# Token halves in one 512-column pass, and two heads of an attention unit issued side by side

## The chip, the cores and the metric

The kernel runs as one launch on one core of a Trainium2 chip. The metric is the device time of that launch in microseconds (us): the median of several runs, lower is better. A difference of about 0.2% (4.6 us) is what a measurement of this kernel can tell from no change.

## The reference

The reference is a small network on 256 tokens of width 1024, all in float32: two layers of a first block, then one layer of a second block. What the change touches is shown; the second block's recurrent mixer is left out.

```python
def swiglu(x, w_gate, w_up, w_down):                       # D_FF = 2816
    return (jax.nn.silu(x @ w_gate) * (x @ w_up)) @ w_down

def first_block(x, ...):
    for layer in range(2):
        x = x + 0.5 * swiglu(rms_norm(x, norm_ffn1[layer]), ...)
        xn = rms_norm(x, norm_mix[layer])
        # 16 heads of 64; layer 0: 8 heads stick-breaking, 8 heads softmax with rotary q, k
        # layer 1: 8 heads softmax with a forgetting term, 8 heads dilated windows with rotary q, k
        mixed = mix(xn, ...)                                # q, k, v = split(xn @ w_in)
        x = x + mixed @ w_out[layer]
        x = x + 0.5 * swiglu(rms_norm(x, norm_ffn2[layer]), ...)
    return x

def peer_ffn(h, w_q, sub_keys, expert_u, expert_v):         # second block, 16384 experts
    ...                                                     # gate, eidx: 8 heads x top 16 of the experts
    act = gelu(einsum('nhed,nd->nhe', expert_u[eidx], hb))
    return einsum('nhe,nhed->nd', gate * act, expert_v[eidx])
```

## The kernel before

Activations lie transposed: a tile `x` of 128 partitions x 8 chunks x 256 tokens. Every large float32 product is made of three passes in the type fp32r: each operand is split into a high part and the remainder, and high x high, high x low and low x high are added up in PSUM. The normalised activations are two tiles, `xnh` and `xnl`; the weights are brought from memory in blocks of 128 x 512 (256 KB) by `wblk`, which loads `wr`, makes `wh` on ScalarE (L195) and `wl` on VectorE or GpSimd (L201). Four blocks rotate, in some stages five.

`ws` is the work horse: for each 128 x 128 weight tile it issues the three passes L224, L225, L226, each with 256 token columns. It serves

- `ffn`, four times: 22 steps of gate and up (both in one PSUM tile `mm`, a "pair" of 2 x 256 columns), evicted by one VectorE multiply with the norm's factor (L297), then SiLU, a multiply and a split into `hh`, `hl`; then 8 output chunks of 22 weight tiles each, evicted by one VectorE instruction (L304);
- `mix`, twice: eight "units" of two heads, in two groups of four. `project` makes q and k of a unit, `heads` normalises and rotates them, `weights` makes scores and softmax (or the stick-breaking weights), `collect` turns the weights round and multiplies by the values. The loop runs them with lags of 1, 2 and 3 units, so that a unit's stages lie beside the projection of later units; `values` makes v once for each group, in passes of 512 columns (L205 to L207);
- `to_x`, the output projection of `mix`, in two parts so that its first half lies beside the last units;
- the 128 steps of the expert stage's `u_phase` (PSUM tile `pu`), 64 of which lie beside the 24 passes of a `v_phase` (L1302 to L1304).

The code gives each engine's work, but a scheduler sets the order on each engine, by its own estimate of when each instruction can run; an instruction under `keep_in_program_order` stays behind the one written before it. Each engine then works its list in order and waits where an operand or a buffer isn't ready. In `mix`, PSUM is four `mm` buffers of one bank and four `w` buffers of one bank, which all attention tiles share in turn (scores, transposes, the two head helpers, the output `O`).

In the attention, head `e` of a unit sits on partitions 64e to 64e + 63 of q and k, so that a score matmul uses 64 of the array's 128 rows; in the product with the values, head `e` fills output partitions 64e to 64e + 63, which is 64 of its columns. These matmuls are plain float32; the profile records each as two.

## Time and profile before

| | |
|---|---|
| median of 3 runs | 2279.07 us (2274.92 to 2279.41) |
| the profiled execution | 2276.94 us, of which the span from first to last instruction 2275.2 us |
| TensorE matmul (PE) busy | 2196.3 us, 97% of the span, 18034 records |
| VectorE (DVE) busy | 1617.6 us, 71% |
| ScalarE (ACT) busy | 1346.1 us, 59% |
| GpSimd (POOL) busy | 283.0 us, 12% |
| mean granted TensorE clock | 0.99 of 2.4 GHz |
| moved by DMA | 365.30 MB, mean 161 GB/s |

Matmul records overlap: one of 256 columns is recorded with some 0.28 us, but the next starts 0.12 us later. So the price of a pass is read from the distance of starts, not from its record, and "busy" on PE also covers short waits.

By stages, in us from the start: first feed-forward 0 to 201, first mix 201 to 343, two feed-forwards 343 to 724, second mix 724 to 870, feed-forward 870 to 1065, the second block's mixer to 1350, its expert stage to 2230, the rest to 2275.

### The profile page before, as it was taken

Reading aid. Unit: us, or ns where it says so; the run is one execution under the profiler, and the core shown is the slowest. Engines: PE = TensorE matmul, PEld = TensorE weight load, DVE = VectorE, ACT = ScalarE, POOL = GpSimd, SP = SyncE. Lnnn points to the kernel's source line nnn. Section 1 sums busy time; section 2 is a strip of 40 time slices with the busy share of each in tenths; the row PEclk is TensorE's granted clock in tenths of the full one; section 3 lists DMA queues with packets and bytes.
Section 4 is the critical chain, followed back from the end, with each engine's and each line's share of the span. In section 5 each row is a group of like instructions: output and inputs, shape, how many; then the busy total and the mean of one; then the engine's idle time right before and its main releaser. Section 6 shows DMA issues by size and latency. Waiting matters only on the chain.

```text
span 2275.2 us, 48212 instructions
## 1 busy us (share of the span) xinstructions
PE 2196.3 (97%) x18034; PEld 2114.0 (93%) x18034; DVE 1617.6 (71%) x3293; ACT 1346.1 (59%) x2667; POOL 283.0 (12%) x272
## 2 busy tenths in 40 slices
PE   8999999999999999999888989889999999999997
PEld 8999889999999789999787889889999999999997
DVE  7766777666766757766886577999996666666666
ACT  6555576556555556556765656456665555555556
POOL 1001100000000101001233027960000000000001
PEclk9999999999999999999998999999999999999999
DMA  6566425565567325565243145443346555555553
GB/s 208 183 181 193 125 94 192 183 183 187 184 179 223 116 83 173 183 181 185 86 134 113 47 156 172 149 140 112 121 144 206 185 185 186 183 189 189 187 186 117
DMA packets 209659, 365.30 MB, mean 161 GB/s; under 512 B 31056, under 2 KB 39312, under 8 KB 208912
## 3 DMA queue, kind: packets, MB, share of 16 engines
q1 hardware_dynamic: 207312, 361.96, 50.4%
q8 instruction: 141, 2.31, 0.4%
q14 instruction: 94, 0.77, 0.1%
q10 hardware_dynamic: 2112, 0.26, 0.1%
HBM read 357.87 MB, written 4.26 MB: 159 GB/s over the span
## 4 chain that ended last, share of the span: by engine, by line
PE 82%; DVE 9%; ACT 3%; DMA 2%; POOL 2%; issue 2%; SPq 0%; DVEq 0%; POOLq 0%; ACTq 0%
PE mm L224 13%; PE mm L226 13%; PE mm L225 13%; PE acc L1302 5%; PE acc L1304 5%; PE acc L1303 5%; PE pu L225 5%; PE pu L224 5%; PE pu L226 5%; DVE wl L201 2%; PE pg L1282 2%; POOL wl L201 1%; DMA wr<-in_pu 1%; PE w L347 1%; PE mm L205 1%
## 5 line engine op out<-in xcount | busy, mean ns | idle before, releaser
L195 ACT ACTIVATE wh<-wr 128x512 fp32r<-128x512 f32 (+1 forms) x1348 | 836.4, 624 | 697.0 <-PE mm L225 240.5
L201 DVE TENSOR_TENSOR wl<-wr,wh 128x512 fp32r<-128x512 f32 (+1 forms) x1234 | 851.6, 696 | 485.5 <-ACT wh L195 455.7
L224 PE MATMUL mm<-xnh,wh 128*128 128x256 f32 x1840 | 529.2, 288 | 10.6 <-ACT wh L195 7.3
L226 PE MATMUL mm<-xnh,wl 128*128 128x256 f32 x1840 | 524.4, 285 | 1.6 <-POOL wl L201 0.9
L225 PE MATMUL mm<-xnl,wh 128*128 128x256 f32 x1808 | 514.7, 285 | 0.1
L224 PEld LDWEIGHTS mm<-xnh,wh 128*128 128x128 f32 x1840 | 355.0, 193 | 15.1 <-ACT wh L195 11.4
L226 PEld LDWEIGHTS mm<-xnh,wl 128*128 128x128 f32 x1840 | 355.0, 193 | 3.9 <-POOL wl L201 1.5
L225 PEld LDWEIGHTS mm<-xnl,wh 128*128 128x128 f32 x1808 | 349.1, 193 | 2.7 <-issue 1.9
L226 PE MATMUL pu<-xnh,wl 128*128 128x256 f32 x1024 | 291.2, 284 | 11.1 <-POOL wl L201 10.6
L224 PE MATMUL pu<-xnh,wh 128*128 128x256 f32 x1024 | 292.9, 286 | 0.0
L225 PE MATMUL pu<-xnl,wh 128*128 128x256 f32 x1024 | 289.6, 283 | 0.0
L1302 PE MATMUL acc<-o,wh 128*128 128x256 f32 x1024 | 286.9, 280 | 0.0
L1304 PE MATMUL acc<-o,wl 128*128 128x256 f32 x1024 | 285.8, 279 | 0.0
L1303 PE MATMUL acc<-o,wh 128*128 128x256 f32 x1024 | 285.7, 279 | 0.0
L226 PEld LDWEIGHTS pu<-xnh,wl 128*128 128x128 f32 x1024 | 195.6, 191 | 13.2 <-POOL wl L201 12.5
L226 PE MATMUL mm<-hh,wl 128*128 128x256 f32 x704 | 197.8, 281 | 0.0
L224 PE MATMUL mm<-hh,wh 128*128 128x256 f32 x704 | 197.1, 280 | 0.0
L224 PEld LDWEIGHTS pu<-xnh,wh 128*128 128x128 f32 x1024 | 196.0, 191 | 0.0
L225 PEld LDWEIGHTS pu<-xnl,wh 128*128 128x128 f32 x1024 | 195.8, 191 | 0.0
L225 PE MATMUL mm<-hl,wh 128*128 128x256 f32 x704 | 195.7, 278 | 0.0
L1304 PEld LDWEIGHTS acc<-o,wl 128*128 128x128 f32 x1024 | 192.4, 188 | 0.1
L1302 PEld LDWEIGHTS acc<-o,wh 128*128 128x128 f32 x1024 | 192.5, 188 | 0.0
(458 smaller groups left out, 3897.7 us busy)
## 6 DMA issues: line engine op xcount, KB each, us to landing
wr<-in_ffn_gu SPq DMA_DIRECT2D x352, 256.0 KB, 2.9
wr<-in_pu SPq DMA_DIRECT2D x256, 256.0 KB, 2.9
wr<-in_pv SPq DMA_DIRECT2D x256, 256.0 KB, 2.9
wr<-in_ffn_d SPq DMA_DIRECT2D x160, 256.0 KB, 2.8
wr<-in_qk SPq DMA_DIRECT2D x64, 256.0 KB, 3.0
wr<-in_wo SPq DMA_DIRECT2D x48, 256.0 KB, 2.9
wr<-in_v SPq DMA_DIRECT2D x32, 256.0 KB, 2.8
wr<-in_u_g SPq DMA_DIRECT2D x32, 256.0 KB, 2.7
```

The costliest lines, as they stand in the source:

```text
L195: nc.scalar.activation(wh[:, :n], wr[:, :n], AF.Copy)
L201: (self.nc.gpsimd if eng == "p" else self.nc.vector).tensor_sub(out, a, b)
L205: nc.tensor.matmul(out, lh, rh, start=start, stop=False)
L224: self.nc.tensor.matmul(out, wh[:, s], h, start=first, stop=False, **kw)
L225: self.nc.tensor.matmul(out, wh[:, s], l, start=False, stop=False, **kw)
L226: self.nc.tensor.matmul(out, wl[:, s], h, start=False, stop=last, **kw)
L347: nc.tensor.matmul(O[s, 0:T], vtok[:, 0, hv * 64:hv * 64 + 64], PT[:, 0:256], start=True, stop=False)
L1282: nc.tensor.matmul(pg[:, j], o[0][:, j], o[1][:, j], start=True, stop=True)
L1302: nc.tensor.matmul(o, vh[:, s], ph, start=first, stop=False, skip_group_check=True)
L1303: nc.tensor.matmul(o, vh[:, s], pl, start=False, stop=False, skip_group_check=True)
L1304: nc.tensor.matmul(o, vl[:, s], ph, start=False, stop=last, skip_group_check=True)
```

## The change

1. `xnh` and `xnl` become the two halves of one tile `xn2`, as `hh` and `hl` become `h2`: for each chunk the 256 high columns and the 256 low columns lie next to each other. A new `ws2` sends both through the array in one pass of 512 columns with the weight tile `wh`, and adds `wl` x high as a pass of 256 columns into the second half of the sum. Three passes become two.
2. The sum then stands in two halves of a PSUM bank; `merged` adds them at eviction: ScalarE copies the second half out, VectorE adds the first half to the copy. Gate/up tiles become `wide` ones of two banks, two in turn instead of four.
3. `ws2` serves gate/up, seven of eight output chunks of each feed-forward, the q and k projections, and 72 of the 128 `u_phase` steps. In the feed-forward the norm's factor goes onto the gate alone and, as `rsh`, onto the output.
4. In `mix`, the score matmuls of a unit's two heads are written in turn (`scores2`), the products with the values too (`pv2`), the transposes head after head (`turn`); all but the first of each series are pinned behind the one before. The transposes become a stage of their own, first in the loop.
5. `to_x` of the first block takes its accumulators from the two wide tiles, four chunks in each; the gates of the second layer and the feed-forward's output chunks use `w` tiles.

```diff
+    def ws2(self, out, src, x2, nk):
+        for b in range(0, nk, self.wk):
+            n = min(self.wk, nk - b)
+            wh, wl = self.wblk(src[:, b * 128:(b + n) * 128], n * 128)
+            for k in range(n):
+                s = slice(k * 128, k * 128 + 128)
+                both = x2[:, b + k].rearrange("p a t -> p (a t)")
+                last = b + k == nk - 1
+                if last:
+                    self.nc.tensor.matmul(out[:, T:], wl[:, s], x2[:, b + k, 0], start=False, stop=False)
+                self.nc.tensor.matmul(out, wh[:, s], both, start=b + k == 0, stop=last)
+                if not last:
+                    self.nc.tensor.matmul(out[:, T:], wl[:, s], x2[:, b + k, 0], start=False, stop=False)
+
+    def merged(self, out, p):
...
+        nc.scalar.activation(c, hi, AF.Copy)
+        nc.vector.tensor_add(out, lo, c)
...
+    def wide(self, tag):
+        return self.ps.tile([128, 2, 2 * T], F32, name=tag, bufs=2)
...
-                p = self.pair("mm")
+                p = self.wide("mm")
                 for j in range(2):
-                    self.ws(p[:, j], gu[f, j], self.xnh, self.xnl, KD)
+                    self.ws2(p[:, j], gu[f, j], self.xn2, KD)
...
-                nc.vector.tensor_mul(s, p, self.rs2())
+                self.merged(s, p)
+                nc.vector.tensor_mul(s[:, 0], s[:, 0], self.rs)
                 nc.scalar.activation(s[:, 0], s[:, 0], AF.Silu)
                 nc.vector.tensor_mul(s[:, 0], s[:, 0], s[:, 1])
-                self.split(hh[:, f], hl[:, f], s[:, 0])
+                self.split(h2[:, f, 0], h2[:, f, 1], s[:, 0])
             for d in range(KD):
-                p = self.pair("mm")
-                self.ws(p[:, 0], dn[d], hh, hl, KF)
-                nc.vector.scalar_tensor_tensor(self.x[:, d], p[:, 0], 0.5, self.x[:, d], op0=ALU.mult, op1=ALU.add)
+                p = self.ps.tile([128, 512], F32, name="w")
+                t = self.tmp.tile([128, T], F32, name="dt")
+                if d < KD - 1:
+                    self.ws2(p, dn[d], h2, KF)
+                    self.merged(t, p)
+                    nc.vector.tensor_mul(t, t, rsh)
+                else:
+                    self.ws(p[:, :T], dn[d], h2[:, :, 0], h2[:, :, 1], KF)
+                    nc.vector.tensor_mul(t, p[:, :T], rsh)
+                nc.vector.tensor_add(self.x[:, d], self.x[:, d], t)
...
+    def scores2(self, q, k, extra=None):
...
+            for n, (l, r) in enumerate(terms):
+                for e in range(2):
+                    i = nc.tensor.matmul(S[e][:, o], l[hs[e], qs], r[hs[e], ks], start=n == 0, stop=n == len(terms) - 1)
+                    if not first:
+                        self.then(i)
...
+        for t, o, c in ((0, slice(0, T), slice(0, 256)), (1, slice(128, T), slice(256, 384))):
+            for e in range(2):
+                i = nc.tensor.matmul(O[hs[e], o], vtok[:, t, vs[e]], PT[e][:, c], start=t == 0, stop=t == 1)
...
-                p = self.pair("mm")
-                self.ws(p[:, 0], A[f"qk_{l}"][c], self.xnh, self.xnl, KD)
-                self.ws(p[:, 1], A[f"qk_{l}"][KD + c], self.xnh, self.xnl, KD)
+                p = self.wide("mm")
+                self.ws2(p[:, 0], A[f"qk_{l}"][c], self.xn2, KD)
+                self.ws2(p[:, 1], A[f"qk_{l}"][KD + c], self.xn2, KD)
                 u["e"] = hd.tile([128, 2, T], F32, name="qk", bufs=4)
-                nc.vector.tensor_mul(u["e"], p, self.rs2())
+                self.merged(u["e"], p)
+                nc.vector.tensor_mul(u["e"], u["e"], self.rs2())
...
-                for lag, stage in ((3, collect), (2, weights), (1, heads)):
+                for lag, stage in ((3, turned), (1, heads), (2, weights), (3, collect)):
...
-            self.to_x(A[f"wo_{l}"], yh, yl, KD, blocks=[4, 0], ahead=4)
+            self.to_x(A[f"wo_{l}"], yh, yl, KD, blocks=[4, 0], ahead=4, wide=True)
...
-                self.ws(p[:, :T], A["pu"][i2], self.xnh, self.xnl, KD)
-                nc.scalar.activation(a, p[:, :T], AF.Gelu)
+                if i2 < self.N0 + self.NX:
+                    self.ws(p[:, :T], A["pu"][i2], self.xnh, self.xnl, KD)
+                    nc.scalar.activation(a, p[:, :T], AF.Gelu)
+                else:
+                    self.ws2(p, A["pu"][i2], self.xn2, KD)
+                    nc.scalar.activation(a, p[:, T:], AF.Copy)
+                    nc.vector.tensor_add(a, a, p[:, :T])
+                    nc.scalar.activation(a, a, AF.Gelu)
```

What it moves on TensorE is seen at two places. The first is gate/up in the first feed-forward; `mm` is the PSUM tile, `wh` and `wl` one weight block's parts. Before:

```order
L224 MATMUL mm_796<-xnh_66,wh_817 128x256
L225 MATMUL mm_796<-xnl_67,wh_817 128x256
L226 MATMUL mm_796<-xnh_66,wl_818 128x256
L224 MATMUL mm_796<-xnh_66,wh_817 128x256
L225 MATMUL mm_796<-xnl_67,wh_817 128x256
L226 MATMUL mm_796<-xnh_66,wl_818 128x256
```

The same place now, at the end of one sum, where the last weight tile's small pass stands ahead of its large one:

```order
L240 MATMUL mm_758<-xn2_66,wh_775 128x512
L242 MATMUL mm_758<-xn2_66,wl_776 128x256
L240 MATMUL mm_758<-xn2_66,wh_775 128x512
L242 MATMUL mm_758<-xn2_66,wl_776 128x256
L239 MATMUL mm_758<-xn2_66,wl_776 128x256
L240 MATMUL mm_758<-xn2_66,wh_775 128x512
L240 MATMUL mm_758<-xn2_66,wh_789 128x512
L242 MATMUL mm_758<-xn2_66,wl_790 128x256
```

Six passes for two weight tiles became four.

The second place is TensorE in the first mix, where one unit's attention stands beside `values` (`mm` with 512 columns). `z` are the softmax weights, `PT` the transposed ones, `qk` q and k of a unit, `hsq` and `c_rot` the two head helpers. Before:

```order
L205 MATMUL mm_3394<-wh_3398,xnh_66 128x512
L206 MATMUL mm_3394<-wl_3399,xnh_66 128x512
L207 MATMUL mm_3394<-wh_3398,xnl_67 128x512
L347 MATMUL w_3333<-PT_3338,vt1_2913 64x256
L348 MATMUL w_3333<-PT_3338,vt1_2913 64x128
L341 MATMUL w_3342<-c_ident_2780,z_3233 128x128
L342 MATMUL w_3342<-c_ident_2780,z_3233 128x128
L343 MATMUL w_3342<-c_ident_2780,z_3233 128x128
L328 MATMUL w_3352<-qk_3195 128x256
L332 MATMUL w_3352<-qk_3195 128x128
L347 MATMUL w_3333<-PT_3346,vt1_2913 64x256
L348 MATMUL w_3333<-PT_3346,vt1_2913 64x128
```

The second head's scores (L328, L332 into `w_3366`) and the two helpers follow. Now:

```order
L503 MATMUL w_2891<-hsq_2889,c_blk_2379 128x512
L508 MATMUL w_2896<-qk_2872,c_rot_2381 128x512
L381 MATMUL w_2903<-qk_2749 128x256
L381 MATMUL w_2904<-qk_2749 128x256
L381 MATMUL w_2903<-qk_2749 128x128
L381 MATMUL w_2904<-qk_2749 128x128
L410 MATMUL w_2931<-PT_2881,vt1_2509 64x256
L410 MATMUL w_2931<-PT_2887,vt1_2509 64x256
L410 MATMUL w_2931<-PT_2881,vt1_2509 64x128
L410 MATMUL w_2931<-PT_2887,vt1_2509 64x128
```

The score matmuls of one head stood between the two heads' products with the values; now the two heads' scores stand together, the products too, and the six transposes (x3 and x3) stand a few passes ahead.

## Rows read from the trace of the kernel before

**Rows 1.** The page's chain that ended last: shares of the span by engine
```profile
PE 82%; DVE 9%; ACT 3%; DMA 2%; POOL 2%; issue 2%; SPq 0%; DVEq 0%; POOLq 0%; ACTq 0%
```

**Rows 2.** Windows: stretch, its us, busy us (records) by engine, clock, DMA
```profile
50.00:100.00 50.00, 50.00 (x419) 50.00 (x418) 34.89 (x62) 28.08 (x52) 0.00 (x0) 1.00 0.57 184
...
248.00:260.00 12.00, 12.00 (x54) 8.51 (x53) 9.30 (x25) 7.74 (x19) 2.59 (x2) 1.00 0.30 93
...
1660.00:1670.00 10.00, 10.00 (x87) 9.91 (x86) 10.00 (x23) 6.23 (x11) 0.00 (x0) 1.00 0.35 109
```

**Rows 3.** Timeline of VectorE in gate/up: start us, us, instruction
```profile
64.57 0.69 DVE L297 TENSOR_TENSOR s<-mm,nrs 128x512 f32<-128x512 f32 x1 [0.15 <-PE mm L226]
...
70.33 0.69 DVE L297 TENSOR_TENSOR s<-mm,nrs 128x512 f32<-128x512 f32 x1 [0.16 <-PE mm L226]
```

**Rows 4.** Timeline of TensorE, end of a feed-forward and `values`
```profile
195.78 0.28 PE L224 MATMUL mm<-hh,wh 128*128 128x256 f32 x1
...
201.08 0.28 PE L224 MATMUL mm<-hh,wh 128*128 128x256 f32 x1
...
201.44 0.40 PE L205 MATMUL mm<-wh,xnh 128*128 128x512 f32 x1
...
211.67 0.39 PE L205 MATMUL mm<-wh,xnh 128*128 128x512 f32 x1
```

**Rows 5.** Timeline of TensorE in the expert stage, a `u_phase` step
```profile
1645.09 0.28 PE L224 MATMUL pu<-xnh,wh 128*128 128x256 f32 x1
...
1647.49 0.28 PE L226 MATMUL pu<-xnh,wl 128*128 128x256 f32 x1
```

**Rows 6.** Timeline of TensorE in the first mix: scores and values products
```profile
226.90 0.71 PE L328 MATMUL w<-qk 64*128 64x256 f32 x4
...
227.76 0.39 PE L224 MATMUL mm<-xnh,wh 128*128 128x256 f32 x1
...
238.58 0.70 PE L328 MATMUL w<-qk 64*128 64x256 f32 x2
...
239.43 0.65 PE L347 MATMUL w<-PT,vt 128*64 128x256 f32 x2
...
240.22 0.70 PE L328 MATMUL w<-qk 64*128 64x256 f32 x2
...
241.07 0.70 PE L436 MATMUL w<-hsq,c_blk 128*128 128x512 f32 x1
```

**Rows 7.** Timeline of TensorE in the second block: its attention's values products
```profile
1263.41 1.09 PE L923 MATMUL mm<-k 128*64 128x256 f32 x8
1264.43 0.27 PE L1135 MATMUL w<-XT,k 64*64 64x64 f32 x1
```

**Rows 8.** Timeline of TensorE in the second mix: scores with the forgetting term
```profile
817.59 0.70 PE L328 MATMUL w<-qk 64*128 64x256 f32 x2
...
818.64 0.65 PE L347 MATMUL w<-PT,vt 128*64 128x256 f32 x2
...
819.44 0.37 PE L332 MATMUL w<-qk 64*128 64x128 f32 x1
...
820.95 0.70 PE L436 MATMUL w<-hsq,c_blk 128*128 128x512 f32 x1
```

**Rows 9.** Groups by line and form: count, busy us, mean ns, idle before
```profile
L299 DVE TENSOR_TENSOR s<-s 128x256 f32<-128x256 f32 x88 | 36.8, 419 | 3.1 <-ACT s L298 3.1
...
L1246 ACT ACTIVATE act<-pu 128x256 f32<-128x256 f32 x90 | 33.0, 367 | 0.0
...
L345 ACT ACTIVATE PT<-w 128x384 f32<-128x384 f32 x32 | 15.5, 484 | 13.3 <-PE w L343 12.9
...
L916 ACT ACTIVATE k<-mm 128x512 f32<-128x512 f32 x8 | 4.7, 586 | 1.5 <-PE mm L914 1.4
```

**Rows 10.** Timeline of TensorE: two waits in the mixes, idle before in brackets
```profile
338.62 0.39 PE L224 MATMUL mm<-yh,wh 128*128 128x256 f32 x1 [2.13 <-DVE x L320]
...
751.18 0.70 PE L436 MATMUL w<-hsq,c_blk 128*128 128x512 f32 x1 [2.42 <-ACT hsq L434]
```

More of the change, by code (lines that the diff above doesn't have):

```diff
@@ L311, in to_x @@
             acc = {}
+            four = None
             for part in ((blocks[:1], blocks[1:]) if ahead else (blocks,)):
@@ L314, in to_x @@
                     if d % 2 == 0 and d not in acc:
-                        p = self.pair(tags[(d // 2) % len(tags)])
+                        if wide and d % 4 == 0:
+                            four = self.wide(tags[0])
+                        p = four[:, d // 2 % 2].rearrange("p (j t) -> p j t", j=2) if wide else \
+                            self.pair(tags[(d // 2) % len(tags)])
                         acc[d], acc[d + 1] = p[:, 0], p[:, 1]
@@ L320, in to_x, with then @@
                         self.nc.vector.tensor_add(self.x[:, d], self.at(x or self.x, d), acc[d])
-    def scores(self, q, k, e, extra=None):
+    def then(self, *ins):
+        for i in ins:
+            self.tc.keep_in_program_order(i)
+    def scores2(self, q, k, extra=None):
         nc = self.nc
-        s = slice(64 * e, 64 * e + 64)
-        S = self.ps.tile([128, 512], F32, name="w")
-        last = extra is None
-        nc.tensor.matmul(S[:, 0:256], q[s, 128:256], k[s, 0:256], start=True, stop=last)
-        if extra is not None:
-            l, r = extra
-            nc.tensor.matmul(S[:, 0:256], l[s, 128:256], r[s, 0:256], start=False, stop=True)
-        nc.tensor.matmul(S[:, 256:384], q[s, 0:128], k[s, 0:128], start=True, stop=last)
-        if extra is not None:
-            nc.tensor.matmul(S[:, 256:384], l[s, 0:128], r[s, 0:128], start=False, stop=True)
+        S = [self.ps.tile([128, 512], F32, name="w") for e in range(2)]
+        hs = [slice(64 * e, 64 * e + 64) for e in range(2)]
+        first = True
+        for o, qs, ks in ((slice(0, 256), slice(128, 256), slice(0, 256)),
+                          (slice(256, 384), slice(0, 128), slice(0, 128))):
+            terms = [(q, k)] + ([] if extra is None else [extra])
+            for n, (l, r) in enumerate(terms):
[3 more added lines that the diff above has]
+                        self.then(i)
+                    first = False
@@ new lines, in pv2 @@
+    def pv2(self, PT, vtok, hv, O):
+        nc = self.nc
+        hs = [slice(64 * e, 64 * e + 64) for e in range(2)]
+        vs = [slice((hv + e) * 64, (hv + e) * 64 + 64) for e in range(2)]
+        first = True
+        for t, o, c in ((0, slice(0, T), slice(0, 256)), (1, slice(128, T), slice(256, 384))):
+            for e in range(2):
+                i = nc.tensor.matmul(O[hs[e], o], vtok[:, t, vs[e]], PT[e][:, c], start=t == 0, stop=t == 1)
+                if not first:
+                    self.then(i)
+                first = False
@@ L404, in mix @@
             LR = []
-            vts, units = {}, [dict(grp=g, pr=pr) for g in self.GORD for pr in range(4)]
+            vts, units = {}, [dict(grp=g, pr=pr, P=[]) for g in self.GORD for pr in range(4)]
             def values(grp):
-                pv = [self.ps.tile([128, 512], F32, name="mm") for t in range(2)]
+                pw = self.wide("mm")
+                pv = [pw[:, t] for t in range(2)]
                 for k in range(KD):
@@ L486, in forget_gates @@
         self.split(wfh, wfl, wf)
-        p = self.pair("mm")
+        p = self.pair("w")
         for k in range(KD):
```

54 lines of the change are left out of this document (30 added, 24 removed).

## Prediction

> **What bounds the kernel now.** I read the chain of waits first: 82% of the span lies on PE, 9% on VectorE [rows 1]. So a gain must shorten TensorE's list, or a loss must make it wait. Then the windows, stage by stage [rows 2]: in gate/up TensorE is busy for 50.00 of 50.00 us, VectorE for 34.89 and ScalarE for 28.08. In the first mix, beside the softmax, TensorE is still full, 12.00 of 12.00, but VectorE has 9.30. At 1660 us, where the expert stage builds its gates, both are full, 10.00 and 10.00. Since a full PE may hide waits, I check the pace by starts. One step of gate/up is 48 passes, and its evictions start at 64.57 and 70.33 us [rows 3]: 5.76 us / 48 = 120.0 ns per 256 columns, the distance at which passes follow each other inside a step, so nothing is lost between steps.
>
> **What two passes instead of three save.** Prices of a pass, all from distances of starts: 256 columns take 120.0 ns in gate/up [rows 3]; in the output chunks, 45 passes from 195.78 to 201.08 us, 117.8 ns; in the expert stage, 20 passes from 1645.09 to 1647.49, 120.0 ns [rows 5]. 512 columns: 45 passes of `values` from 201.44 to 211.67 us, 227.3 ns [rows 4]. Thus 512 columns are 12.7 ns cheaper than two passes at 120.0, and 8.3 ns cheaper than two at 117.8. The weight-tile groups that go from three to two passes: gate/up 4 x 22 x 2 x 8 = 1408, q and k 2 x 8 x 2 x 8 = 256, `u_phase` 72 x 8 = 576, together 2240 at 12.7 ns = 28.4 us; output chunks 4 x 7 x 22 = 616 at 8.3 ns = 5.1 us. Sum **33.5 us**. Bounds: if a 256 pass next to a 512 one runs at 117.8 in the first three too, 2240 x 2.2 ns = 4.9 us more, 38.4; if 512 columns beside changing weights cost 2 x 117.8 = 235.6 ns, only 2240 x 4.4 ns = 9.9 us. I take the measured middle, as `values` changes its weights at each pass as well.
>
> The Trainium skill speaks against this term: "TensorE: Matmul & The Clock Gate", section "Back-to-back issue gap", gives the start distance as the columns at the granted clock plus some 2.5 ns, so that joining two passes would save only these, an estimate of 2856 x 2.5 ns = 7 us. This trace disagrees: at a granted clock of 1.00 [rows 2] 256 columns are 106.7 ns of 2.4 GHz cycles, and 120.0 or 117.8 are measured [rows 3, 4]; a pass has 11 to 14 ns of its own here.
>
> **What hides the new eviction.** Per step of gate/up ScalarE gets a copy of 512 columns, 0.59 us by the nearest row [rows 9]; VectorE's multiply of 512 columns, 0.69 us, becomes an add of the same size, and a multiply of 256 comes on top, 0.42 us [rows 9]. Scaled from the windows to a step of 5.55 us: VectorE 34.89/50 x 5.76 + 0.42 = 4.44 us, 80%; ScalarE 3.23 + 0.59 = 3.82, 69%. Both stay below TensorE, and with two wide tiles the eviction has a whole step to end in. I cost it at nothing. The last output chunk gets one more VectorE instruction ahead of the next norm, 0.42 us, four times; the next stage's passes on other chunks cover part: **-1 us** (bounds 0 and -1.7).
>
> In the expert stage the last eight of the `u_phase` steps ahead of `v_phase` fall where VectorE is full; each adds an add of 0.42 us and takes only 8 x 12.7 ns from TensorE. That is up to -3.4 us; windows at the end of the stage have some room: **-2 us**. Beside `v_phase` VectorE isn't near its limit.
>
> **What pairing saves.** Where the two heads' scores happen to stand together, they run side by side: the first unit's four matmuls take 227.76 - 226.90 = 0.86 us. Where another kind stands between, each head takes that alone: 239.43 - 238.58 = 0.85 and 241.07 - 240.22 = 0.85 [rows 6]. A pair saves 0.84. With the forgetting term, the heads take 818.64 - 817.59 = 1.05 and 820.95 - 819.44 = 1.51 us [rows 8], 2.56 in all; side by side I estimate the 1.51 that one whole head needs, so 1.05 saved. In each mix one unit is already together. Scores: 7 + 3 units x 0.84 + 4 x 1.05 = 12.6 us. The values products take 240.22 - 239.43 = 0.79 us for one head [rows 6]. Whether two run side by side on 64 columns each, the second block shows: 8 records of 256 columns in 1264.43 - 1263.41 = 1.02 us [rows 7], 0.13 a record, where one head alone needs 0.79 us for two records of 256 and two of 128 columns, 0.26 for each 256. So a unit's products take 0.79 instead of 1.58: 16 x 0.79 = 12.6 us. Sum **25.2 us**, which is the upper bound.
>
> Against it stand three things. (a) In the rotary units VectorE has 9.30 us per 12.00 [rows 2] and gets 0.69 more, 9.99, while TensorE's 12.00 become 12.00 - 1.63 - 0.2 = 10.2. Nothing waits by this sum, but a margin of 0.2 us won't stay free: **-3 us** over both mixes. (b) In the units without rotation, transposes, scores and products now stand with little between them, and the products wait for ScalarE's copies of 0.48 us [rows 9], covered by scores of 0.86 us unless a weight cast is ahead: 8 units x 0.4 = **-3 us** (0 to -6). (c) In `to_x` four chunks share a PSUM tile, and a pass into it waits until VectorE has added the chunk before; already in pairs one such wait was 2.13 us [rows 10]. Of 8 chunks, 6 instead of 4 now have one, with passes of the other tile between them: 2 x 1.5 = **-3 us** (0 to -8.5).
>
> The scheduler also puts TensorE's rows of the second block's mixer into another order in places; no row prices that, I take nothing, and 4 us either way for the range.
>
> **The sum.** 33.5 + 25.2 - 1 - 2 - 3 - 3 - 3 = 46.7 us. From the execution's own 2276.94 us that is 2230.2. The median of the runs, 2279.07, is 2.1 above this execution, so I predict **2232 us**. The best case of all terms is 38.4 + 25.2 + 4 = 68 us, 2211; the worst of this case, with 9.9 and half the pairing and all losses (1.7 + 3.4 + 3 + 6 + 8.5 + 4), is -4 us, no change.
>
> **Rivals.** *Evacuation takes the pairing's gain.* VectorE or ScalarE become the bound of the mixes, which keep their pace of before: 33.5 - 3 - 3 = 27.5 us, 2252 by the median. For it: the margin of 0.2 us above and in-order queues. Against it: only the rotary units are that full. The Trainium skill's "TensorEngine Tiling (Array Packing)", "Performance Considerations", warns of just this, that packing speeds up the array but not what empties PSUM; VectorE at 9.30 of 12.00 agrees that it is near.
>
> *The pass gain is not there.* A pass of 512 between passes of 256 costs as much as two, the lower bound: 9.9 + 25.2 - 12 = 23 us, 2256. Against it is the even 227.3 ns of `values`.
>
> *Slower.* TensorE's queue is in order, and what is pinned can't be filled with weight passes. If each unit's transposes or products wait for softmax weights that come late, every pass behind them waits. The trace has a wait of 2.42 us of that kind, before L436 [rows 10]. It decides at 46.7 / 16 = 2.9 us of new waiting per unit; at 5 us, half of such a unit's time, the kernel takes 2279 - 47 + 80 = 2312. Against it: the stages keep their lag of a unit or more, and the softmax of a unit has some 10 us.
>
> *It does nothing.* Would need both gains eaten at once, by (c) and the new order in the mixer.
>
> **Chances.** The forecast with its own range of 2217 to 2246: 0.70. Evacuation: 0.14. No pass gain: 0.08. Slower: 0.05. Nothing: 0.03. The range that leaves out no more than 2 in 10 takes in the evacuation case: 2217 to 2256. Faster by over 0.2% (4.6 us, about what a measurement of this kernel can tell from no change): 0.92; within it 0.03; slower 0.05.
>
> **What the profile after would show.** Gate/up evictions some 5.55 us apart instead of 5.76; passes L240 followed by L242 after 227 ns, and the reverse after 118 to 120; scores and products of a unit within about 0.86 and 0.79 us; the first mix shorter by 10 us or more; a `u_phase` step 0.10 us shorter. I am wrong if 512-column passes are more than 235 ns apart, if TensorE's idle time in the mixes names VectorE or ScalarE with more than some 1 us per unit, or if the transition from `to_x` to the feed-forward grows by more than 4 us per layer.

## The result and the profile after

The changed kernel takes 2250.61 us (median of 4 runs, 2247.32 to 2252.97) against 2279.24 for the kernel before: a ratio of 0.9877, 95% interval 0.9857 to 0.9897, 28.6 us faster. The profiled execution took 2247.32 us (span 2245.5), 29.6 less than the one before. 46.7 us less were forecast: the direction held, the gain is three fifths of that. The time lies outside the forecast's own range (2217 to 2246 us) and inside the wide one (2217 to 2256), which had been stretched to take in the evacuation rival.

By stages, in us, cut at the starts of TensorE's first and last passes of each; the four right columns are versions that the experiments come to:

| stage | before | after | passes alone | pairs alone | lag 4 | weights below |
|---|---|---|---|---|---|---|
| four feed-forwards | 769.2 | 756.9 | 755.5 | 769.1 | 755.0 | 752.1 |
| two mixes of the first block | 286.8 | 273.6 | 289.8 | 270.2 | 268.8 | 269.4 |
| second block's mixer | 303.7 | 305.5 | 303.2 | 299.5 | 305.1 | 302.2 |
| expert stage up to `v_phase` | 323.5 | 325.3 | 325.3 | 324.7 | 324.5 | 326.7 |
| `v_phase` | 543.6 | 537.5 | 539.6 | 543.6 | 537.5 | 526.6 |
| rest | 48.1 | 46.6 | 48.1 | 47.3 | 48.1 | 46.8 |

So the feed-forwards gave 12.3 us, the mixes 13.2, `v_phase` 6.2; the rest cost 2.1.

The chain of the page after, as [rows 1]: TensorE's share fell by 4 points, VectorE's rose by 2.

```profile
PE 78%; DVE 11%; ACT 3%; DMA 2%; issue 2%; POOL 2%; SPq 0%; DVEq 0%; POOLq 0%; ACTq 0%
```

Windows of the same kind as [rows 2] (busy us and records of TensorE, its weight loads, VectorE, ScalarE, GpSimd; granted clock; DMA share, GB/s). The second stretch is the rotary part of the first mix:

```profile
50.00:100.00 50.00, 50.00 (x286) 43.50 (x285) 37.81 (x72) 33.17 (x63) 0.00 (x0) 1.00 0.59 186
236.00:248.00 12.00, 9.28 (x54) 6.43 (x52) 9.13 (x34) 8.55 (x25) 2.56 (x2) 1.00 0.30 87
```

Gate/up is still full; the mix no longer is: 9.28 of 12.00 us, where it was 12.00 [rows 2]. The evictions in the second feed-forward, 18 steps apart (first fence), and those of its output chunks, 6 apart (second), answer [rows 3, 4]:

```profile
357.30 0.69 DVE L251 TENSOR_TENSOR s<-mm,mg 128x512 f32<-128x512 f32 x1 [0.76 <-ACT mg L250]
...
458.82 0.69 DVE L251 TENSOR_TENSOR s<-mm,mg 128x512 f32<-128x512 f32 x1 [0.76 <-ACT mg L250]
```

```profile
466.33 0.42 DVE L251 TENSOR_TENSOR dt<-w,mg 128x256 f32<-128x256 f32 x1
...
512.21 0.42 DVE L251 TENSOR_TENSOR dt<-w,mg 128x256 f32<-128x256 f32 x1
```

A step takes 101.52 / 18 = 5.640 us, a group of one 512 and one 256 pass 352.5 ns (three passes: 360.0, forecast 347.3). In the output chunks it is 45.88 / 6 / 22 = 347.6 ns (before 353.3, forecast 345.1). By the distances of starts the 512 pass takes 235.6 ns in gate/up and 229 in the output chunks, the 256 pass 117 and 118.

The pairs run side by side, as [rows 6] answers here:

```profile
238.03 0.52 PE L394 MATMUL w<-c_ident,z 128*128 128x128 f32 x3 [1.50 <-ACT mg L250]
...
242.08 0.92 PE L381 MATMUL w<-qk 64*128 64x256 f32 x8
...
242.94 0.87 PE L410 MATMUL w<-PT,vt 128*64 128x256 f32 x8
243.74 0.50 PE L240 MATMUL mm<-xn,wh 128*128 128x512 f32 x1
...
248.16 0.55 PE L394 MATMUL w<-c_ident,z 128*128 128x128 f32 x3 [1.37 <-DVE z L428]
```

By the distances of starts, both heads' scores take 0.86 us (242.94 - 242.08) and both heads' products 0.80 (243.74 - 242.94). But ahead of the transposes (L394, which read the softmax weights `z`) TensorE now waits. Groups in the windows of the first and the second mix (idle time before them and its releasers at the end):

```profile
L394 PE MATMUL w<-c_ident,z 128*128 128x128 f32 x48 | 8.1, 285 | 6.6 <-ACT z L445 3.8 <-ACT mg L250 1.5 <-DVE z L428 1.4
...
L503 PE MATMUL w<-hsq,c_blk 128*128 128x512 f32 x8 | 4.4, 637 | 1.0 <-ACT hsq L501 1.0
...
L503 PE MATMUL w<-hsq,c_blk 128*128 128x512 f32 x16 | 8.8, 629 | 1.1 <-ACT hsq L501 1.1
L394 PE MATMUL w<-c_ident,z 128*128 128x128 f32 x48 | 8.1, 280 | 4.4 <-ACT mg L250 1.5 <-ACT z L425 1.5 <-DVE z L428 1.3
```

In the kernel before, the transposes had 0.1 and 0.3 us of idle time. Windows over both mixes, before and then after:

```profile
201.40:340.10 138.70, 134.97 (x874) 114.40 (x873) 98.36 (x212) 89.58 (x191) 15.55 (x16) 1.00 0.39 125
718.80:867.20 148.40, 144.64 (x946) 121.25 (x946) 100.12 (x256) 90.48 (x207) 16.68 (x16) 1.00 0.40 129
```

```profile
199.40:333.50 134.10, 123.33 (x750) 99.17 (x750) 98.01 (x221) 91.43 (x198) 15.65 (x15) 1.00 0.42 133
706.00:845.80 139.80, 132.64 (x817) 105.13 (x817) 100.03 (x264) 94.47 (x216) 16.12 (x15) 1.00 0.43 137
```

TensorE's busy time fell from 279.6 to 256.0 us, by 23.6; its idle time rose from 7.5 to 17.9, by 10.4. The difference is the 13.2 us.

### The profile page after: what moved, and what is told of

It is laid out like the page before. It is cut to its first block, busy times and chain, and to the rows that moved or that the text cites. A ratio compares the mean times of both kernels' runs of the same rounds, so it can differ in the third digit from the quotient of the medians.

```text
span 2245.5 us, 43202 instructions
## 1 busy us (share of the span) xinstructions
PE 2148.4 (96%) x15178; PEld 1940.4 (86%) x15178; DVE 1682.2 (75%) x3533; ACT 1431.7 (64%) x2873; POOL 286.3 (13%) x272
## 4 chain that ended last, share of the span: by engine, by line
PE 78%; DVE 11%; ACT 3%; DMA 2%; issue 2%; POOL 2%; SPq 0%; DVEq 0%; POOLq 0%; ACTq 0%
PE mm L240 16%; PE mm L242 7%; PE w L240 6%; PE pu L240 5%; PE acc L1376 5%; PE acc L1378 5%; PE acc L1377 5%; PE w L242 3%; PE pu L242 2%; PE pu L225 2%; DVE wl L201 2%; PE pu L226 2%; PE pu L224 2%; PE pg L1356 1%; DVE o L1352 1%
## 5 line engine op out<-in xcount | busy, mean ns | idle before, releaser
L240 PE MATMUL mm<-xn,wh 128*128 128x512 f32 x1664 | 579.3, 400 | 8.9 <-ACT wh L195 8.2
L242 PE MATMUL mm<-xn,wl 128*128 128x256 f32 x1456 | 411.9, 283 | 0.8 <-DVE wl L201 0.8
L240 PEld LDWEIGHTS mm<-xn,wh 128*128 128x128 f32 x1664 | 301.2, 189 | 67.9 <-ACT wh L195 8.8
L1376 PE MATMUL acc<-o,wh 128*128 128x256 f32 x1024 | 286.7, 280 | 0.0
L242 PEld LDWEIGHTS mm<-xn,wl 128*128 128x128 f32 x1456 | 276.2, 190 | 11.8 <-DVE wl L201 2.0
L1378 PE MATMUL acc<-o,wl 128*128 128x256 f32 x1024 | 286.1, 279 | 0.0
L240 PE MATMUL w<-h,wh 128*128 128x512 f32 x616 | 212.7, 391 | 0.0
L240 PE MATMUL pu<-xn,wh 128*128 128x512 f32 x576 | 207.6, 396 | 0.0
L1377 PEld LDWEIGHTS acc<-o,wh 128*128 128x128 f32 x1024 | 191.6, 187 | 3.2 <-DVE o L177 0.2
L1378 PEld LDWEIGHTS acc<-o,wl 128*128 128x128 f32 x1024 | 192.8, 188 | 0.0
L1376 PEld LDWEIGHTS acc<-o,wh 128*128 128x128 f32 x1024 | 192.2, 188 | 0.0
L201 POOL TENSOR_TENSOR wl<-wr,wh 128x512 fp32r<-128x512 f32 x114 | 166.8, 1485 | 80.7 <-ACT wh L195 69.2
L282 POOL TENSOR_TENSOR sq<-sq 128x256 f32<-128x256 f32 x56 | 48.1, 858 | 875.3 <-ACT sq L280 429.0
L242 PE MATMUL pu<-xn,wl 128*128 128x256 f32 x504 | 139.8, 277 | 0.0
L226 PE MATMUL pu<-xn,wl 128*128 128x256 f32 x448 | 127.9, 286 | 12.4 <-POOL wl L201 11.2
L240 PEld LDWEIGHTS w<-h,wh 128*128 128x128 f32 x616 | 113.9, 188 | 22.6
L224 PE MATMUL pu<-xn,wh 128*128 128x256 f32 x448 | 129.1, 288 | 0.0
L225 PE MATMUL pu<-xn,wh 128*128 128x256 f32 x448 | 126.8, 283 | 0.0
## 6 DMA issues: line engine op xcount, KB each, us to landing
wr<-in_ffn_gu SPq DMA_DIRECT2D x352, 256.0 KB, 2.9
wr<-in_pu SPq DMA_DIRECT2D x256, 256.0 KB, 2.9
wr<-in_pv SPq DMA_DIRECT2D x256, 256.0 KB, 3.0
wr<-in_ffn_d SPq DMA_DIRECT2D x160, 256.0 KB, 2.9
wr<-in_qk SPq DMA_DIRECT2D x64, 256.0 KB, 3.1
wr<-in_wo SPq DMA_DIRECT2D x48, 256.0 KB, 2.9
wr<-in_v SPq DMA_DIRECT2D x32, 256.0 KB, 2.8
wr<-in_u_g SPq DMA_DIRECT2D x32, 256.0 KB, 2.7
```

The source lines that it names most:

```text
L201: (self.nc.gpsimd if eng == "p" else self.nc.vector).tensor_sub(out, a, b)
L224: self.nc.tensor.matmul(out, wh[:, s], h, start=first, stop=False, **kw)
L225: self.nc.tensor.matmul(out, wh[:, s], l, start=False, stop=False, **kw)
L226: self.nc.tensor.matmul(out, wl[:, s], h, start=False, stop=last, **kw)
L240: self.nc.tensor.matmul(out, wh[:, s], both, start=b + k == 0, stop=last)
L242: self.nc.tensor.matmul(out[:, T:], wl[:, s], x2[:, b + k, 0], start=False, stop=False)
```

## Experiments

Two questions are open. Why does a group save 7.5 ns in gate/up and not 12.7? Theory 1: the 227.3 ns of a 512 pass, read in `values` [rows 4], were the wrong price beside 256 passes on another operand. And where does the mixes' idle time come from? Theory 2: from the transposes' place right behind a softmax that is late. Its rival: VectorE and ScalarE have become the bound of these stretches.

**Each part alone.** The first version is the changed kernel with the attention of before, the second the kernel before with `scores2`, `turn`, `pv2` and the new order of stages.

```diff
-    def scores2(self, q, k, extra=None):
-    def turn(self, P, C):
-    def pv2(self, PT, vtok, hv, O):
+    def scores(self, q, k, e, extra=None):
+    def pv(self, P, vtok, hv, O, e, C):
...
-                for lag, stage in ((3, turned), (1, heads), (2, weights), (3, collect)):
+                for lag, stage in ((3, collect), (2, weights), (1, heads)):
```

> Two passes for three alone; the attention of the kernel before (scores, transposes and values products head by head, nothing pinned). Theory 1, that the price of the pass was mis-sized (a group of two passes takes 353 ns in gate/up, not 347.3, against 360 before) and that the parts hardly touch: the feed-forwards as in the changed kernel (about 12 us shorter in sum), the expert stage 6 us shorter, the mixes 0 to 3 us shorter, so 2258 to 2263 in all, 16 to 21 us under the kernel before. Rival, that the pass gain is whole (33 us) and the new attention took it back: 2245 to 2249.

> The paired attention alone; three passes as before. Theory 1, that the pairs run side by side (scores 0.85 us and values products 0.85 us per unit, some 23 us in both mixes) but the transposes, now standing together ahead of them, wait for the softmax weights: the mixes together 10 to 14 us shorter, 2265 to 2270 in all, with 4 to 7 us of idle time per mix ahead of the transposes. Rival, that the waits come from the slower eviction of q and k (a copy and an add more) and not from the attention's order: with the old eviction no idle time ahead of the transposes, the mixes 20 us or more shorter, 2259 or less.

Passes alone: 2263.6 us, ratio 0.9937 (0.9924 to 0.9951), 14.3 us faster. The rival of the first run (2245 to 2249) falls; theory 1's time is just missed, since the expert stage gave 2.2 us and not 6, and the mixes got longer. Pairs alone: 2261.78, ratio 0.9933 (0.9920 to 0.9947), 16.1 faster. The sum, 30.4, is about the 28.6 of both, so the parts hardly touch. Windows over the mixes, passes alone and then pairs alone:

```profile
198.00:339.50 141.50, 134.38 (x750) 106.70 (x749) 103.15 (x221) 92.16 (x198) 15.74 (x15) 1.00 0.40 127
711.90:860.50 148.60, 143.38 (x818) 113.06 (x817) 105.37 (x264) 94.10 (x216) 16.33 (x15) 1.00 0.41 129
```

```profile
201.20:333.20 132.00, 123.56 (x874) 105.93 (x874) 93.34 (x212) 87.75 (x191) 15.46 (x16) 1.00 0.43 131
711.90:850.30 138.40, 132.94 (x946) 112.54 (x946) 94.10 (x256) 89.40 (x207) 16.50 (x16) 1.00 0.44 139
```

Passes alone: TensorE's busy time in the mixes falls by 1.9 us (256 groups of 7.2 ns), its idle time grows by 4.8; the mixes get 3.0 us longer, which no theory had. VectorE has 10.0 us more there (208.5 for 198.5), ScalarE 6.2. Pairs alone: 23.1 us less busy, 6.4 more idle, and with the old eviction 4.9 and 2.0 us of it still stand ahead of the transposes: the attention's order makes waits of its own, so the rival of the second run falls. The mixes gained 16.7 us and the whole 16.1, both between the two expectations.

**The transposes' wait.** Three versions of the changed kernel: another order of the stages, a whole unit more between softmax and transposes, and transposes that wait for no softmax at all.

```diff
-                for lag, stage in ((3, turned), (1, heads), (2, weights), (3, collect)):
+                for lag, stage in ((1, heads), (3, turned), (2, weights), (3, collect)):   # heads first
+                for lag, stage in ((4, turned), (1, heads), (2, weights), (4, collect)):   # lag 4
...
-                u["PT"] = self.turn(u["P"], C)
+                u["PT"] = self.turn([C["mcausal"]] * 2, C)                                 # no softmax wait
```

> The changed kernel with the stages of a unit's round written as heads, turned, weights, collect (instead of turned first), so that the six transposes stand behind the two helper products of the next unit. Theory 2: the transposes wait for softmax weights that are late by 0.5 to 1.9 us (6.6 and 4.4 us in the two mixes); behind the helpers the softmax of the rotary units has some 2 us more: those waits go, the units without rotation (no helpers in the first layer) keep theirs; 3 to 6 us less, 2245 to 2248. Rival, that the wait only moves on, to the values products behind their copies: within 2 us of the changed kernel's 2250.6.

> The changed kernel with transposes and values products a whole unit later (lag 4 instead of 3, seven buffers for the softmax weights instead of five, one more round at the end). Theory 2: nearly no idle time is left ahead of the transposes except in the last units, where no projection follows; 5 to 9 us less, 2242 to 2246. Rival, that VectorE and ScalarE set the pace of a unit with the pairs side by side: the idle time stays, ahead of other instructions, within 2 us of 2250.6.

> The changed kernel in which the transposes read a finished constant (the causal mask) instead of the softmax weights; the softmax is computed all the same and its result left out. Theory 2: the mixes lose the 11 us of idle time ahead of the transposes, some 9 to 12 us less in all (mixes 129 and 135 us instead of 134.0 and 139.6). Rival, that VectorE and ScalarE are the bound of these stretches: at most 3 us less.

Heads first: 2247.84 us, ratio 0.9867 (0.9852 to 0.9882), which overlaps the changed kernel's. Lag 4: 2244.36, ratio 0.9851 (0.9836 to 0.9866), 6 us less than the changed kernel, though the two intervals still touch; its mixes took 4.8 us less. No softmax wait: 2242.84 in one run, but its mixes took 272.2 us, only 1.4 less than the changed kernel's, where 9 to 12 were expected. Groups of both mixes with lag 4 (first fence) and without the softmax wait (second fence):

```profile
L394 PE MATMUL w<-c_ident,z 128*128 128x128 f32 x48 | 7.1, 274 | 1.0 <-ACT wh L195 1.0
L503 PE MATMUL w<-hsq,c_blk 128*128 128x512 f32 x8 | 4.5, 644 | 3.8 <-ACT hsq L501 3.8
...
L503 PE MATMUL w<-hsq,c_blk 128*128 128x512 f32 x16 | 9.0, 645 | 3.8 <-ACT hsq L501 3.8
```

```profile
L394 PE MATMUL w<-c_ident,c_mcausal 128*128 128x128 f32 x48 | 6.9, 276 | 1.0 <-DVE z L434 1.0
L503 PE MATMUL w<-hsq,c_blk 128*128 128x512 f32 x8 | 4.5, 645 | 3.8 <-ACT hsq L501 3.8
...
L503 PE MATMUL w<-hsq,c_blk 128*128 128x512 f32 x16 | 9.4, 667 | 4.7 <-ACT hsq L501 4.5
```

The 11.0 us ahead of the transposes fall to 1.1 in both, and 7.6 us (lag 4) or 8.5 us (no softmax wait) now stand ahead of the helper product L503, where the changed kernel has 2.1; L503 waits for ScalarE's square of the freshly evicted q and k. So theory 2 is right on the place, and lag 4's time is the one it forecast; but over half of the idle time that was taken away comes back as a wait for the eviction of the next unit, so the worth of that wait is less than its length, as the rivals said. Heads first does the same (3.6 and 0.0 us ahead of the transposes, 3.7 and 4.0 ahead of L503); in its profile TensorE stood more in the last units, and the granted clock was 0.50 (1.2 GHz) from 320 to 328 us, behind a stretch with 2.24 busy of 4.00 us (first fence). The changed kernel's profile has 1.98 of 4.00 in the same stretch and stayed at 1.00 (second fence), so how full that stretch was does not by itself tell when the clock falls:

```profile
316.00:320.00 4.00, 2.24 (x12) 1.51 (x12) 3.93 (x8) 1.71 (x4) 0.00 (x0) 0.85 0.21 66
320.00:324.00 4.00, 3.02 (x11) 1.74 (x11) 0.04 (x1) 1.30 (x3) 0.00 (x0) 0.50 0.02 4
```

```profile
316.00:320.00 4.00, 1.98 (x13) 1.51 (x13) 2.92 (x6) 1.54 (x3) 0.00 (x0) 1.00 0.20 70
```

**Three passes for q and k again, with lag 4.** Theory 4 took the 3.0 us of the first run for the price of the new eviction.

```diff
-                self.ws2(p[:, 0], A[f"qk_{l}"][c], self.xn2, KD)
+                self.ws(p[:, 0], A[f"qk_{l}"][c], self.xnh, self.xnl, KD)
...
-                self.merged(u["e"], p)
-                nc.vector.tensor_mul(u["e"], u["e"], self.rs2())
+                nc.vector.tensor_mul(u["e"], p, self.rs2())
```

> The changed kernel with transposes and products a unit later (as in the earlier run with lag 4, 2244.4 us) and, new, with q and k made by three passes again and evicted by one VectorE multiply, as in the kernel before. Theory 4: in the mixes the two passes cost more in eviction (ScalarE and VectorE work queued ahead of the softmax) than they save on TensorE; alone they made the mixes 3.0 us longer: the mixes 3 to 6 us shorter than with lag 4 alone (130.4 and 138.4), 2239 to 2242 in all. Rival, that with lag 4 that work is hidden: TensorE gets 256 groups of 7 ns back, 2 us longer or more, 2246 to 2248.

2244.76 us, ratio 0.9863 (0.9844 to 0.9883): no difference from lag 4 that can be told. The mixes of its profile took 275.5 us, where lag 4 has 269.0 and 3 to 6 less were expected. Theory 4 falls as far as it promised a gain; the 2 us or more of its rival are not shown either. In its mixes VectorE has 10.5 us less than with lag 4, and TensorE still 13.4 us of idle time (granted clock 0.97 in the first mix, 1.00 in the second), so the sum of VectorE's work isn't what sets it; which instruction of that chain does is open.

**The price of a group.** First 32 idle bytes ahead of the normalised tile, or behind it, which shifts operands and weights:

```diff
+        self.pad = self.const.tile([128, 8], F32, name="pad")        # ahead
         self.xn2 = self.const.tile([128, KD, 2, T], F32R, name="xn2")
+        self.pad = self.const.tile([128, 8], F32, name="pad")        # or behind
```

> The changed kernel with 32 idle bytes per partition ahead of the tile of normalised activations, so that it and everything behind it (weights, the feed-forward's hidden tile) move by 32. Why does a group take 353 ns in gate/up and 347 in the output chunks? If the start address of the moving operand alone decides (it is a multiple of 64 for the normalised tile, 32 past one for the hidden tile): gate/up 347, output chunks 353, about 9 us less in all. If the distance between moving operand and weights decides: no change. If the busier VectorE and ScalarE decide: no change.

> The changed kernel with the 32 idle bytes behind the tile of normalised activations: it stays, weights and hidden tile move by 32. If the distance between moving operand and weights decides (both start at 256 past a multiple of 2048 now; the hidden tile starts 32 further): gate/up 347 instead of 353 ns a group, output chunks unchanged at 347, 10 to 14 us less in all. If the moving operand's address alone decides: gate/up unchanged at 353, output chunks 353, 4 us more. If the busier engines decide: no change.

2255.43 and 2246.7 us, single runs whose totals say little, and the group's price hardly changed: 352.5 ns in gate/up and 347.6 in the output chunks with the pad ahead, 352.9 and 347.6 with the pad behind. The evictions with it behind, 18 steps apart:

```profile
356.35 0.69 DVE L253 TENSOR_TENSOR s<-mm,mg 128x512 f32<-128x512 f32 x1 [0.76 <-ACT mg L252]
...
457.99 0.69 DVE L253 TENSOR_TENSOR s<-mm,mg 128x512 f32<-128x512 f32 x1 [0.76 <-ACT mg L252]
```

Then the traffic beside the passes:

```diff
+        if self.mode == "none":
+            return self.fix[1], self.fix[2]
...
+        if self.mode == "cast":
+            wr = self.fix[0]
+        else:
+            nc.sync.dma_start(wr[:, :n], src)
+        if self.mode == "load":
+            nc.scalar.activation(self.fix[0][:, :1], wr[:, :1], AF.Copy)
+            return self.fix[1], self.fix[2]
```

> The changed kernel with less weight work beside the same passes in gate/up, from the fifth step on: in the first feed-forward all passes use one block that was loaded and split once (no loads, no splits); in the second the split is made anew for each block but from one loaded block (no loads); in the third each block is loaded but the passes use one split block (no splits); the fourth is as before. The other weights' products are left out. Theory 3, that the 353 ns of a group in gate/up (347 in the output chunks) come from engines or transfers that work on the on-chip memory beside TensorE: 340 to 348 in the first feed-forward, and the second and third tell which of the two it is. Rival, that the pair of passes costs this by itself: 352 to 354 in all four.

Windows in its first three feed-forwards, and evictions of the first, 13 steps apart:

```profile
60.00:110.00 50.00, 50.00 (x285) 43.49 (x285) 16.94 (x36) 12.96 (x27) 0.00 (x0) 1.00 0.00 1
380.00:430.00 50.00, 50.00 (x286) 43.47 (x285) 38.07 (x72) 33.22 (x62) 0.00 (x0) 1.00 0.00 1
570.00:620.00 50.00, 48.86 (x276) 41.96 (x274) 20.59 (x41) 21.34 (x69) 0.00 (x0) 1.00 0.72 235
```

```profile
64.61 0.69 DVE L269 TENSOR_TENSOR s<-mm,mg 128x512 f32<-128x512 f32 x1 [2.61 <-ACT mg L268]
...
138.01 0.69 DVE L269 TENSOR_TENSOR s<-mm,mg 128x512 f32<-128x512 f32 x1 [2.61 <-ACT mg L268]
```

With DMA at 0.00 and VectorE busy for a third of the time, a group still takes 73.40 / 13 / 16 = 352.9 ns; with loads and no splits, the third, TensorE waited for loads now and then. Theory 3 falls.

Then the form of the passes, one in each feed-forward:

```diff
+                x2 = hp.tile([128, KD, 2, T], F32R, name="xc")
+                for k in range(KD):
+                    nc.scalar.activation(x2[:, k], self.xn2[:, k].bitcast(F32), AF.Copy)
...
+                    p = [self.ps.tile([128, 512], F32, name="w") for j in range(2)]
...
+                    self.ws2(p[j], gu[f, j], x2, KD, first=case != 2 or j == 0, end=case != 2 or j == 1, large_first=case == 3)
...
+                    self.ws2(p, dn[d], self.xn2 if case == 1 else h2, KF, mod=8 if case == 1 else 99, cut=8 if case == 2 else 99, large_first=case == 3)
```

> The changed kernel with another form of the two passes in each of the four feed-forwards, to find what makes a group (one 512 and one 256 pass) take 353 ns in gate/up and 347 in the output chunks. First: gate/up sums in two tiles of one bank, output sums in the two-bank tile. Second: gate/up passes read a copy of the normalised activations that lies behind the hidden tile, output passes read the normalised tile (so their products are other ones). Third: gate/up adds up 16 groups in one sum instead of 8 (gate and up in one), output chunks start a new sum every 8 groups (again other products). Fourth: the four 512 passes of a weight block stand first, then the four 256 passes. Whichever of these decides makes gate/up 347 or the output chunks 353 in its own feed-forward and leaves 353 and 347 in the others: PSUM tile (first), moving operand (second), length of the sum (third), alternation of sizes (fourth, where values with 512 passes alone suggests 340 to 347 in both places). Rival: none of them, 353 and 347 in all four.

In the first (other PSUM tiles) gate/up and output chunks took 352.5 and 347.5 ns a group, in the third (longer and shorter sums) 353.4 and 349.4. In the fourth (large passes first) the two prices met, at 349.6 and 350.3; its gate/up, 19 steps apart:

```profile
870.98 0.69 DVE L265 TENSOR_TENSOR s<-mm,mg 128x512 f32<-128x512 f32 x1 [1.07 <-ACT mg L264]
...
977.25 0.69 DVE L265 TENSOR_TENSOR s<-mm,mg 128x512 f32<-128x512 f32 x1 [1.07 <-ACT mg L264]
```

In the second, gate/up (19 steps) and then output chunks (4):

```profile
358.76 0.69 DVE L265 TENSOR_TENSOR s<-mm,mg 128x512 f32<-128x512 f32 x1 [0.73 <-ACT mg L264]
...
464.91 0.69 DVE L265 TENSOR_TENSOR s<-mm,mg 128x512 f32<-128x512 f32 x1 [0.73 <-ACT mg L264]
```

```profile
480.06 0.42 DVE L265 TENSOR_TENSOR dt<-w,mg 128x256 f32<-128x256 f32 x1
...
511.14 0.42 DVE L265 TENSOR_TENSOR dt<-w,mg 128x256 f32<-128x256 f32 x1
```

From the copy behind the hidden tile a gate/up group takes 349.2 ns; the output chunks rise to 353.2 when they read the normalised tile. So the moving operand decides most of the difference, and short sums add some 2 ns. It is not alone: the other order of passes takes 2.9 ns off gate/up, nearly as much as the copy (3.3), and adds 2.7 to the output chunks. Why is open.

Is it the operand's place, or that of the weights too?

```diff
+            if case == 0:
+                x2 = hp.tile([128, KD, 2, T], F32R, name="xc")
             h2 = hp.tile([128, KF, 2, T], F32R, name="h2")
+            if case > 1:
+                x2 = hp.tile([128, KD, 2, T], F32R, name="xc")
+            if case in (1, 2):
+                self.wp, self.wx = E.enter_context(tc.tile_pool(name="wp2", bufs=4)), None
...
+                        self.ws(p[:, 0, j * T:j * T + T], gu[f, j], x2[:, :, 0], x2[:, :, 1], KD)
```

> The earlier run showed that the moving operand decides: from a copy that lies behind the hidden tile (byte 118048 of each partition) a gate/up group took 349.3 ns, from the normalised tile (byte 10496; the weights lie from 26880 to 57600) 353, and the output chunks rose to 353.3 when they read that tile. Is it the place of the operand itself or its nearness to the weights? All gate/up of the changed kernel, a form in each feed-forward. First: the copy just behind the working tiles, at byte 72992. Second: the normalised tile in its place, weights from a pool at 118048. Third: copy at 118048, weights from a pool behind it, at 134432. Fourth: copy at 118048, three passes of 256 as in the kernel before, which took 360 a group there. Theory 5a, the low place itself is slower: 349 in the first, 353 in the second, 349 in the third. Theory 5b, operand and weights near each other are slower: 349 in the first, 349 in the second, 353 in the third. Both: 353 to 356 in the fourth, which would say that 4 to 7 ns of the 360 of before were the same place and not a price of passes. Rival: place has no part in it, the copy's single writer has (ScalarE alone writes it): 349 in the first and third, 353 in the second, as 5a; then the hidden tile, written by two engines and at 347, speaks against it.

Evictions in its four feed-forwards, 14, 18, 18 and 18 steps apart:

```profile
62.64 0.69 DVE L251 TENSOR_TENSOR s<-mm,mg 128x512 f32<-128x512 f32 x1 [0.73 <-ACT mg L250]
...
140.86 0.69 DVE L251 TENSOR_TENSOR s<-mm,mg 128x512 f32<-128x512 f32 x1 [0.73 <-ACT mg L250]
...
360.89 0.69 DVE L251 TENSOR_TENSOR s<-mm,mg 128x512 f32<-128x512 f32 x1 [0.76 <-ACT mg L250]
...
462.52 0.69 DVE L251 TENSOR_TENSOR s<-mm,mg 128x512 f32<-128x512 f32 x1 [2.20 <-ACT mg L250]
...
550.17 0.69 DVE L251 TENSOR_TENSOR s<-mm,mg 128x512 f32<-128x512 f32 x1 [0.75 <-ACT mg L250]
...
651.68 0.69 DVE L251 TENSOR_TENSOR s<-mm,mg 128x512 f32<-128x512 f32 x1 [2.19 <-ACT mg L250]
...
879.92 0.41 DVE L352 COPY s<-mm 128x256 f32<-128x256 f32 x1
...
980.72 0.41 DVE L352 COPY s<-mm 128x256 f32<-128x256 f32 x1
```

A group takes 349.2, 352.9, 352.5 and, with three passes, 350.0 ns. So 5a alone fails (slow in the third, at a high place) and 5b alone fails (slow in the second, far from the weights); common to the slow ones is that the operand lies at a lower address than the weights. The rival falls too: the third reads the copy that ScalarE alone wrote, and is slow. And with the operand moved, three passes cost 350.0 ns instead of 360: two instead of three save 0.8 ns there.

**Weights below the operand**, lag 4 otherwise:

```diff
+        wp = c.enter_context(tc.tile_pool(name="wp", bufs=4))
         P = Prog3(c, tc, A)
-        P.wp = c.enter_context(tc.tile_pool(name="wp", bufs=4))
+        P.wp = wp
```

> The version with lag 4 (2244.4 us), in which the four weight buffers lie ahead of the normalised tile in each partition (bytes 1152 to 25728, the tile from 35072) instead of behind it; same instructions. In the earlier runs a group took 353 ns wherever the moving operand lay at a lower address than the weights (10496 under 35072; under 126240; 118048 under 142624) and 347 to 349 wherever it lay above them. Theory 5c, that this order decides: 349 to 350 in gate/up for four of five blocks (the fifth buffer still lies above), 4 us less in the feed-forwards, 1 in the mixes, and some 3 to 7 in the expert stage and the second block, whose passes read the same tile: 2232 to 2237. Rival, that it is another property of these places (the low part of the memory, or certain distances): 352 to 353 as before, 2241 to 2247.

2229.66 us, ratio 0.9796 (0.9777 to 0.9816): 14.7 us less than lag 4, 21 less than the changed kernel, and the best version here. Gate/up (18 steps, first fence) gives 350.5 ns, near the forecast of 5c for four of five buffers. But the largest gain, 10.8 us, came in `v_phase`. First and last of 24 passes L1376 to L1378, with lag 4 (second fence) and then here (third):

```profile
351.06 0.69 DVE L251 TENSOR_TENSOR s<-mm,mg 128x512 f32<-128x512 f32 x1 [0.73 <-ACT mg L250]
...
452.00 0.69 DVE L251 TENSOR_TENSOR s<-mm,mg 128x512 f32<-128x512 f32 x1 [0.74 <-ACT mg L250]
```

```profile
1990.59 0.28 PE L1376 MATMUL acc<-o,wh 128*128 128x256 f32 x1
...
1993.30 0.28 PE L1378 MATMUL acc<-o,wl 128*128 128x256 f32 x1
```

```profile
1989.56 0.28 PE L1376 MATMUL acc<-o,wh 128*128 128x256 f32 x1
...
1992.18 0.28 PE L1378 MATMUL acc<-o,wl 128*128 128x256 f32 x1
```

2.71 / 23 = 117.8 ns a pass became 2.62 / 23 = 113.9, although its operand `o` lay above the weights in both, by the order in which the kernel opens its pools. The time came out below the 2232 to 2237 that 5c forecast, and its rule, order alone, is not what makes it. That place decides is shown; which property of the places is open.

## Why the forecast was right in sign and too large in size

- **Two passes for three, 33.5 us: the term that was mis-sized.** Measured: feed-forwards 12.3 (gate/up 1408 x 7.5 = 10.6 and output chunks 616 x 5.7 = 3.5, less 1.8 that is left over for the stages' ends), q and k 1.9, `v_phase` 6.2: some 20 us, 13 less than forecast, which is most of the 18 us by which the whole gain fell short. The step that failed took the 512 price from `values` [rows 4] and the 256 price from gate/up [rows 3]. In `values` the weights are the moving operand, in gate/up the activations, and the two lie in different places: the 12.7 ns were at least in part a difference of places. Beside 256 passes in gate/up a 512 pass takes 235.6 ns, which is the forecast's lower bound and just past its own sign of being wrong (235); that the 256 pass fell to 117 made it 7.5 ns a group and not 4.4. In `v_phase` the price did come: 360.3 ns a group became 348.1. But in the versions passes alone and heads first, whose code for this stage is the same, it was 352.6, for a reason that stays open.
- The Trainium skill's "TensorE: Matmul & The Clock Gate", "Back-to-back issue gap", gives its 2.5 ns for a pass by itself; of a stream of weight loads and matmuls, which this kernel is, it says that both together set the spacing. 2.5 ns per pass saved lie between the 0.8 measured with both forms on the same copy and the 5.7 to 12.2 of the other places, and the start distances that the rule gives (columns at the clock plus 2.5 ns) agree with no row here.
- **Eviction hidden: right in gate/up** (VectorE 37.81 of 50.00 us, forecast 80%), **wrong in the mixes**, where 4.8 us of idle time came with it.
- **Pairing, 25.2 us: right.** TensorE's busy time in the mixes fell by 23.1 us with pairs alone; 0.86 and 0.80 us per unit (forecast 0.86 and 0.79).
- **Against it, 9 us: the sum near, by luck, as one term was too large and two were too small.** Idle time grew by 10.4 us. (a), a squeeze in the rotary units, came to 4.8 us, the waits there growing from 3.0 to 7.8. (b) put 3 us into the units without rotation, behind ScalarE's copies and ahead of the products; the products have 0.0 us, but TensorE waits 5.4 us for the same units one step earlier, ahead of the transposes (0.8 us in all before): 3.8 us of the first mix's wait ends with L445, the last step of the stick-breaking weights. (c), `to_x`, was the wrong way round: waits for VectorE's additions there fell from 3.1 to 1.1 us. The first mix became 4.6 us shorter, where 10 or more were forecast.
- **Evacuation as a rival** (2252 us) came within 2 us of the time, and that is luck: it had the mixes keep their pace and the passes give 33.5 us, while the mixes gave 13.2 and the passes some 20. In part the mixes did become what it says, since 10.4 of the 23.6 us went into waits. The Trainium skill's "TensorEngine Tiling (Array Packing)", "Performance Considerations", warns that packing speeds up TensorE and not what empties PSUM; the waits here agree in that they are for the engines behind PSUM, but they are for single results that come late, not for a full engine (VectorE is busy for 98.01 of 134.10 us).
- The last eight `u_phase` steps (-2 us) and the second block's mixer (0, 4 either way): 1.8 us longer each. The mixer took 299.5 to 305.5 us in versions with the same code for it, so its 1.8 says nothing.

## What to carry over

Take both prices of a comparison from the same operand in the same place, since here two places of one tile differed by more than two forms of the same work. When TensorE's work is packed more densely, look for the next wait twice: remove the first one by experiment and see whether the time goes or only moves on. Where SBUF has room, try another order of the pools: three moved lines gave half of what the whole change gave (14.7 of 28.6 us).

## What was not expected of the hardware

- The distance of passes depends on where moving operand and weights lie in SBUF: 360 or 350 ns for three passes of 256 columns in gate/up, and, with the same instructions throughout, 117.8 or 113.9 ns a pass in `v_phase`. A shift by 32 bytes changed the group in gate/up by 0.4 ns at most, and taking away all DMA and over half of VectorE's and ScalarE's work there did not change it either (352.9 ns).
- At the end of the first mix TensorE now has stretches half idle, and behind one the granted clock fell to 0.50 in the profile of heads first (the mean over that mix was 0.96; 1.00 in the changed kernel's, with a stretch as idle).
